# Weight-block sums moved to the input projection, and the start of the output projection rearranged, in a two-layer decoder kernel

## The chip, the core and the metric

The kernel runs on one NeuronCore of a Trainium2 chip. Its engines work side by side, each through its own list of instructions in order: TensorE (PE; PEld are its weight loads), VectorE (DVE), ScalarE (ACT), GpSimd (POOL), and SyncE (SP), which here issues nearly all DMA transfers (SPq is its queue). They wait for one another by semaphores. The metric is the device time of one launch in microseconds, the median of several runs; before the change it is 2179.95 us (2179.53 to 2179.99 in 3 runs).

## The reference

The program is a trunk of two decoder layers over 1024 positions of width 1024, in float32. Layer 0 mixes by latent attention with 12 heads, layer 1 by a sliding window of 128 with 12 query heads and 4 key heads; both have four more heads that attend to a memory of 256 rows.

```
for i in range(DEPTH):
    hn = rmsnorm(x, attn_norm_g[i])
    if i % 2 == 0:
        mix, q_cross = mla_mixer(hn, positions, mla_w_in[j], ..., mla_w_uq[j], mla_w_ukv[j])
    else:
        mix, q_cross = swa_mixer(hn, positions, swa_w_in[j], swa_sinks[j])
    cross = memory_cross_attention(q_cross, mem_n, w_mem_kv[i])
    x = x + jnp.concatenate([mix, cross], axis=-1) @ w_o[i]
    x = x + squared_relu_mlp(rmsnorm(x, mlp_norm_g[i]), mlp_w_up[i], mlp_w_down[i])
return rmsnorm(x, final_norm_g)
```

In the mixer of layer 0, queries come from a product of rank 384 with `mla_w_uq`, of which 64 columns of each head are used as they are and 32 are rotated by position (rope).

## The kernel before

**Products.** A float32 product is made of three fast ones: each operand is split into a high part (a rounding copy, line 99, on ScalarE) and a low part (a subtraction, line 100, on VectorE), and TensorE adds high x high, high x low and low x high in PSUM. A split is thus one operation on ScalarE and, after it, one on VectorE.

**The output projection** `@ w_o` (`wo_phase`) and the MLP use a Strassen-like scheme: 2x2 blocks, seven block products (numbered 1 to 7, done in the order 1, 5, 6, 3, 2, 7, 4), each of which takes sums of blocks as operands. A block product is four steps over the inner dimension (28 steps in all, four PSUM blocks of 128x512 each), and the results go to two sets of four banks, `pswy` (Y) and `pswz` (Z); when a product is complete, VectorE adds the banks to the token tiles (line 1264). The operands of step n are made by `prep(n)`, five steps ahead.

**The weight-block sums** (`wo_sums`, lines 607 to 640) prepare four of the seven weight operands ahead of time and put them, split, into DRAM (`wt_5h`, `wt_5l` and so on). The work is cut into eight quarters. A quarter is 4 loads of w_o (8 in layer 1, whose rows are permuted by head), 4 subtracts (lines 625 to 628), 4 splits and 8 stores. All quarters use one set of four buffers, so the loads of the next quarter wait until the stores of the last have landed. The generator is advanced by `next(summing)` at chosen places:

- in layer 0, two steps for each tile of the values stage (a loop over 8 tiles, in which also the cross attention runs, `pscx`, `pscT`, `psco`) and for each block of the keys (`pskn`); its buffers `wos` are a pool of their own, `wop`, released behind the keys. In the place of `wop` the pool `wu2` opens, with the rope's scratch tiles `ra` and `rb` (lines 299 to 304) and some query weights.
- in layer 1, two steps for each half of a job of the input projection, from the job n = 3 on. A job takes 128 columns of `swa_w_in` (loaded as `wsr`, line 1902; its high and low parts are `wf`). The buffers are the first half of `f1`, which the first score blocks of the window attention (`psw`, with its probabilities `p` in `f1`, line 2009) use next.

**Stages of layer 0, in order of time:** norms and memory products (to about 50 us); the input projection (`psin`, one tile of 128 tokens after another; `psT_a` transposes the normalised tokens, whose split is `xhls`; then the norm of the latent vectors, lines 172 to 184 and 561 to 563, the rope of the key, lines 299 to 304, and `psct` transposes the result); values and cross; keys; the rope queries (`psqr`, then rope on VectorE and POOL, then the transposes `psqt`); attention (`pss`, `pso`); output projection; MLP.

**Around the output projection of layer 0.** The last head's sums of probabilities are handled apart (`LastHead`): ScalarE copies out its denominator and its 64 rows for each half of the tokens (lines 999 and 1002), SP spreads the denominators over partitions, VectorE multiplies. The tokens for the residual come by three groups of loads (line 1202), the first MLP weights by `fill_w` at steps 16 and 18, scaled by ScalarE (line 1362) and split. Behind the last steps the tokens are normalised (`norm`) and transposed (`xT_`).

**What sets the order.** The instructions of each engine are put in order ahead of time by a scheduler that follows the program and the priorities given in it; tiles get their memory from pools, and a new tile waits for the last use of what lay in its place.

## Time and profile before

| | before |
|---|---|
| median of the runs | 2179.95 us |
| the profiled execution | 2177.83 us |
| its span, first to last instruction | 2176.1 us |
| TensorE busy, granted clock | 2080.5 us, 0.982 |
| VectorE busy | 1556.4 us (72%) |
| ScalarE busy | 1149.4 us (53%) |
| GpSimd busy | 161.5 us (7%) |
| HBM read and written | 206.34 MB and 93.63 MB |

The profile is taken from one execution. A row of a timeline has the start and the duration in us, the engine, the line of the kernel, the instruction with output<-input, how many of them, and in brackets the engine's idle time before it and what ended it. What released a wait is inferred from semaphores. The granted clock is the share of its full speed that TensorE was given. A busy engine off the path costs nothing; idle time of TensorE, busy 96% of the span, mostly does.

### The profile page before, as it was taken

To read this page: it belongs to the slowest core of one execution; us is meant where nothing else is said; L and a number is where in the kernel's file an instruction comes from. 1 tells how busy PE (TensorE), PEld (TensorE's weight loads), DVE (VectorE), ACT (ScalarE), POOL (GpSimd) and SP (SyncE) were. 2 spreads that over 40 slices of the span, in tenths; PEclk is the share of its full clock that TensorE was granted. 3 is DMA by queue.
4 is the path that set the end of the run, shared out by engine and by line. 5 is a ranking of instruction groups with operands and counts; after the bars stand their busy time and mean duration, and the time that the engine had idled before them with its cause. 6 is when DMAs were issued, how large, how long until landed. Compare 5 with 4: busy or idle time off the path is not lost.

```text
span 2176.1 us, 29775 instructions
## 1 busy us (share of the span) xinstructions
PE 2080.5 (96%) x9832; PEld 1700.2 (78%) x9832; DVE 1556.4 (72%) x3013; ACT 1149.4 (53%) x2504; POOL 161.5 (7%) x224
## 2 busy tenths in 40 slices
PE   7998699999999999999999999799999999999998
PEld 6987578777777788888888878568778888888887
DVE  7567478867886767795657566687987677886665
ACT  5445367865754444444445453785854444444452
POOL 0012100000100000000001133350000000000000
PEclk9999799999999999999999999899999999999999
DMA  7116323337254445963533235318154445954342
GB/s 250 56 45 184 105 56 94 91 111 242 91 163 147 132 159 174 322 218 114 176 114 112 69 104 155 96 44 285 59 186 139 159 160 176 326 185 145 126 119 90
DMA packets 209797, 314.44 MB, mean 144 GB/s; under 512 B 21629, under 2 KB 101994, under 8 KB 209642
## 3 DMA queue, kind: packets, MB, share of 16 engines
q1 hardware_dynamic: 203200, 296.77, 42.8%
q0 software_dynamic: 4016, 13.12, 1.7%
q10 hardware_dynamic: 2426, 2.65, 0.4%
q8 instruction: 77, 1.26, 0.2%
q14 instruction: 78, 0.64, 0.1%
HBM read 206.34 MB, written 93.63 MB: 138 GB/s over the span
## 4 chain that ended last, share of the span: by engine, by line
PE 60%; DMA 13%; DVE 9%; ACT 5%; issue 2%; SPq 1%; POOL 0%; DVEq 0%; ACTq 0%
PE psy L1799 5%; PE psy L1801 5%; PE psy L1800 5%; DMA mr<-in_mlp_w_up_dram 4%; PE psz L1799 4%; PE psz L1800 4%; PE psz L1801 4%; PE pss L917 4%; PE pso L959 3%; DMA d<-in_mlp_w_up_dram 3%; PE psu L1462 3%; PE psu L1463 3%; PE psu L1464 3%; PE psv L1464 1%; PE psv L1463 1%
## 5 line engine op out<-in xcount | busy, mean ns | idle before, releaser
L1362 ACT ACTIVATE mr<-mr,gcol 128x256 f32<-128x256 f32 (+1 forms) x160 | 67.4, 476 | 83.0 <-DMA mr<-in_mlp_w_up_dram 72.0
L1362 ACT ACTIVATE d<-d,gcol 128x256 f32<-128x256 f32 x128 | 57.2, 498 | 84.1 <-DMA d<-in_mlp_w_up_dram 59.6
L1799 PE MATMUL psy<-g 128*128 128x512 f32 x256 | 99.9, 390 | 0.0
L1800 PE MATMUL psy<-g 128*128 128x512 f32 x256 | 99.6, 389 | 0.0
L1801 PE MATMUL psy<-g 128*128 128x512 f32 x256 | 99.3, 389 | 0.0
L99 ACT ACTIVATE g<-i 128x512 fp32r<-128x512 f32 x79 | 49.6, 628 | 88.0 <-PE psz L1800 45.2
L100 DVE TENSOR_TENSOR g<-i,g 128x512 fp32r<-128x512 f32 x79 | 55.7, 705 | 49.3 <-ACT g L99 49.2
L99 ACT ACTIVATE uh<-i 128x512 fp32r<-128x512 f32 x66 | 41.6, 631 | 85.2 <-PE psy L1800 40.7
L938 ACT ACTIVATE p<-pss 128x512 f32<-128x512 f32 x108 | 63.6, 593 | 43.5 <-PE pss L917 43.4
L99 ACT ACTIVATE i<-mr 128x512 fp32r<-128x512 f32 x78 | 49.0, 628 | 69.0 <-PE psy L1800 20.4
L100 DVE TENSOR_TENSOR pl<-p,ph 128x512 fp32r<-128x512 f32 (+1 forms) x96 | 61.7, 652 | 26.4 <-ACT ph L99 25.9
L789 DVE TENSOR_REDUCE m<-psx 128x1 f32<-128x128 f32 (+5 forms) x96 | 70.3, 749 | 11.1 <-PE psx L785 10.8
L100 DVE TENSOR_TENSOR uh<-i,uh 128x512 fp32r<-128x512 f32 x66 | 45.5, 690 | 45.0 <-ACT uh L99 44.9
L1799 PE MATMUL psz<-g 128*128 128x512 f32 x192 | 74.7, 389 | 0.0
L1800 PE MATMUL psz<-g 128*128 128x512 f32 x192 | 74.7, 389 | 0.0
L1801 PE MATMUL psz<-g 128*128 128x512 f32 x192 | 74.7, 389 | 0.0
L100 DVE TENSOR_TENSOR i<-mr,i 128x512 fp32r<-128x512 f32 x78 | 53.6, 688 | 21.6 <-ACT i L99 21.3
L99 ACT ACTIVATE ph<-p 128x512 fp32r<-128x512 f32 (+1 forms) x96 | 56.4, 599 | 1.3
L1680 DVE TENSOR_TENSOR mqf<-mqq,mqf 128x512 f32<-128x512 f32 x64 | 43.1, 686 | 19.3 <-DMA mqq<-in_mlp_w_down_dram 19.1
L1801 PEld LDWEIGHTS psy<-g 128*128 128x128 f32 x256 | 48.0, 188 | 10.1
L1799 PEld LDWEIGHTS psy<-g 128*128 128x128 f32 x256 | 48.1, 188 | 9.9
L1800 PEld LDWEIGHTS psy<-g 128*128 128x128 f32 x256 | 48.1, 188 | 9.8
(685 smaller groups left out, 7006.2 us busy)
## 6 DMA issues: line engine op xcount, KB each, us to landing
i<-hd SPq DMA_DIRECT2D x154, 256.0 KB
hd<-uh SPq DMA_DIRECT2D x76, 256.0 KB
hd<-ul SPq DMA_DIRECT2D x76, 256.0 KB
mr<-in_mlp_w_up_dram SPq DMA_DIRECT2D x36, 512.0 KB
hd<-x SPq DMA_DIRECT2D x72, 256.0 KB
mr<-hd SPq DMA_DIRECT2D x70, 256.0 KB
d<-in_mlp_w_up_dram SPq DMA_DIRECT2D x32, 512.0 KB
mqq<-in_mlp_w_down_dram SPq DMA_DIRECT2D x32, 512.0 KB
```

The source lines that it names most:

```text
L99: r = nc.scalar.activation(hi, src, AF.Copy)
L100: nc.vector.tensor_tensor(lo, src, f32(hi), ALU.subtract)
L789: nc.vector.reduce_max(m8s[h][:, i : i + 1], ps[:, c], axis=AX, negate=True)
L917: return lambda: nc.tensor.matmul(o, a, b, skip_group_check=True, **kw)
L959: mms.append(lambda: nc.tensor.matmul(o, a, b, skip_group_check=True, **kw))
L1362: nc.scalar.activation(w[:, k, :], w[:, k, :], AF.Copy, scale=g_mlp[layer][:, k0 + k : k0 + k + 1])
L1462: nc.tensor.matmul(ps, wh[:, k, :], xh[:, k, :], start=p in (1, 2, 5) and k == 0, stop=False, skip_group_check=True)
L1463: nc.tensor.matmul(ps, wh[:, k, :], xl[:, k, :], start=False, stop=False, skip_group_check=True)
L1464: nc.tensor.matmul(ps, wl[:, k, :], xh[:, k, :], start=False, stop=k == 3, skip_group_check=True)
L1799: nc.tensor.matmul(ps, ah[:, j, :], bh, start=p in (1, 5, 2) and k == 0, stop=False, skip_group_check=True)
L1800: nc.tensor.matmul(ps, ah[:, j, :], bl, start=False, stop=False, skip_group_check=True)
L1801: nc.tensor.matmul(ps, al[:, j, :], bh, start=False, stop=k == NP - 1, skip_group_check=True)
```

## The change

Four groups of edits:

1. *Sums of layer 0.* They move ahead, into the loop of the input projection (two steps per iteration from the second on), with four buffers and four places for high parts in the second half of `f1`. The pool `wop` goes.
2. *Sums of layer 1.* They start at job 4 instead of 3, with two sets of four buffers in the first half of `f1` and three places for high parts in a small pool `wosp`.
3. *Output projection.* The first two left operands are split before the attention's end (`woa`, in steps 8 and 9 of `WoRaw`). In layer 0, Y takes single banks and Z pairs (the other way round before). The last head's normalisation covers 128 rows at once, instead of 64 here and 64 by `rc_mul(3)`. The token loads `a5` and `u2` move to steps 1 and 6; the first MLP weights are loaded and scaled at steps 2 and 4 instead of 16 and 18, and split at 6 and 14; tokens are normalised at steps 20 and 21 and their first transposes start at step 21. Product 4's weight operands have a tile of their own.
4. *MLP start.* Two transposes instead of three are left to the MLP, and a scaling (`gain_w(0)`) comes behind the last split of the output projection.

```
+    quarters = [f1[:, 2 + i // 4, (i % 4) * 256 : (i % 4) * 256 + 256] for i in range(8)]
+    summing = wo_sums(0, [quarters[0:4]], quarters[4:8])
     a_norm(0)
     for k in range(NT + 2):
+        for _ in range(2 if k else 0):
+            next(summing, None)
...
+        def run():
+            for n in range(ns):
+                load(n)
+            yield
+            for n in range(8):
+                s = sets[n % ns]
+                V(s[0], s[1], s[0], ALU.subtract)
+                V(s[1], s[2], s[1], ALU.subtract)
+                V(s[2], s[2], s[0], ALU.subtract)
+                V(s[3], s[3], s[2], ALU.subtract)
+                put(n, 0)
+                put(n, 1)
+                yield
+                put(n, 2)
+                put(n, 3)
+                if n + ns < 8:
+                    load(n + ns)
+                yield
...
-    wop = pool("wop", "right")
-    summing = wo_sums(0, wop.tile([P, 6, 256], F32, name="wos"))
...
         values_of(t)
-        for _ in range(2):
-            next(summing, None)
...
-        for _ in range(2):
-            next(summing, None)
         nc.vector.tensor_copy(kn[j][:, 0:512], ps[:, 0:512])
...
-    wop.release()
...
+            if n in (8, 9):
+                t_ = quad.tile([P, 2, 512], F32R, tag="raw", bufs=2, name=f"woa{self.layer}_{n}")
+                self.a.append([t_[:, e, :] for e in range(2)])
+                self.his.append(split(self.o[:, 2 * (n - 8), 0:512], *self.a[-1]))
...
-            if n == GRP[c + 1] * NB + LB + 3:
+            if c < 3 and n == GRP[c + 1] * NB + LB + 3:
                 muls = rc_mul(c)
...
         load(a1, 0, 0)
-        load(a5, 1, 1)
-        load(u2, 0, 1)
...
-        for n in range(4):
-            prep(n)
+        with tc.high_priority(offset=150):
+            for n in range(4):
+                prep(n)
         if head:
-            with tc.issue_after(his[1].ins):
+            with tc.issue_after(his[3].ins):
                 head()
...
+        Y, Z = banks("y", layer == 1), banks("z", layer == 0)
...
+            if n == 1:
+                load(a5, 1, 1)
+            if n == 6:
+                load(u2, 0, 1)
...
-            if n in (16, 18):
-                m.fill.append(fill_w(layer, m, n // 2 - 8))
+            if n in (2, 4):
+                fills.append(fill_w(layer, m, n // 2 - 1))
+            if n in (6, 14):
+                m.fill.append(fills[n // 14]())
...
-            if p == 7:
-                norm(n % 4)
+            if n in (20, 21):
+                norm(2 * (n - 20))
+                norm(2 * (n - 20) + 1)
+            if n > 20:
+                xT_(n - 21)
...
-        m.late = [lambda t=t: xT_(t) for t in (5, 6, 7)]
+        m.late = [lambda t=t: xT_(t) for t in (6, 7)]
...
-            if n == 3 and not i:
-                summing = wo_sums(1, f1[:, 0:2, :].rearrange("p a (b c) -> p (a b) c", c=256))
-            for _ in range(2 if n > 2 else 0):
+            if n == 4 and not i:
+                quarters = [f1[:, i_ // 4, (i_ % 4) * 256 : (i_ % 4) * 256 + 256] for i_ in range(8)]
+                wosp = pool("wosp")
+                wos = wosp.tile([P, 3, 256], F32, name="wos")
+                summing = wo_sums(1, [quarters[0:4], quarters[4:8]], [wos[:, e, :] for e in range(3)])
+            for _ in range(2 if n > 3 else 0):
                 next(summing, None)
```

Three places show how the built order of the instructions moves.

VectorE, one tile of layer 0's input projection, before: from the split of the next tile (`xhls`), through the norm's small steps (lines 183, 184), to the normalised tokens (line 201) and latent vectors (561, 562).

```order
L100 TENSOR_TENSOR xhls<-psT_a_0_1092,xhls 128x512
L183 TENSOR_SCALAR ss_1106<-ss_1106 128x1
L183 TENSOR_SCALAR ss_1039<-ss_1039 128x2
L340 SCALAR_TENSOR_TENSOR qc_88<-psct_0_1069,qc_88 64x128
L184 TENSOR_TENSOR rs_1110<-rs_1110,ss_1106 128x1
L184 TENSOR_TENSOR rs_1045<-rs_1045,ss_1039 128x2
L100 TENSOR_TENSOR xhls<-psT_a_4_1099,xhls 128x512
L201 TENSOR_SCALAR fa_86<-fa_86,rs_1110 128x1024
L561 TENSOR_SCALAR fa_87<-psin_990,rs_1045 128x384
L562 TENSOR_SCALAR fa_87<-psin_990,rs_1045 128x256
```

The same place in the changed kernel; lines 620 to 622 are three of the subtracts of the sums, whose quarters are parts of the tile `fa_87`.

```order
L620 TENSOR_TENSOR fa_87<-fa_87 128x256
L183 TENSOR_SCALAR ss_1098<-ss_1098 128x1
L183 TENSOR_SCALAR ss_1007<-ss_1007 128x2
L621 TENSOR_TENSOR fa_87<-fa_87 128x256
L184 TENSOR_TENSOR rs_1102<-rs_1102,ss_1098 128x1
L184 TENSOR_TENSOR rs_1013<-rs_1013,ss_1007 128x2
L340 SCALAR_TENSOR_TENSOR qc_88<-psct_0_1037,qc_88 64x128
L201 TENSOR_SCALAR fa_86<-fa_86,rs_1102 128x1024
L561 TENSOR_SCALAR fa_87<-psin_958,rs_1013 128x384
L562 TENSOR_SCALAR fa_87<-psin_958,rs_1013 128x256
L340 SCALAR_TENSOR_TENSOR qc_88<-psct_0_1037,qc_88 64x128
L622 TENSOR_TENSOR fa_87<-fa_87 128x256
```

Subtracts stand inside the chain of the norm now; the two splits of `xhls` have left it and stand behind the rope that follows these rows.

TensorE at the start of layer 0's output projection, before (with buffer numbers): the last matmul of the attention, then the first blocks of the first product (lines 1258 to 1260); `pswy0_0` is a tile of two banks, so the first two blocks go to it.

```order
L959 MATMUL pso11_0_4962<-pl11_0_3_4973,vh1_2695 128x384
L1258 MATMUL pswy0_0_5084<-wob0_4788,g0_0_13_5043 128x512
L1259 MATMUL pswy0_0_5084<-wob0_4788,g0_0_13_5043 128x512
L1260 MATMUL pswy0_0_5084<-wob0_4788,g0_0_13_5043 128x512
L1258 MATMUL pswy0_0_5084<-wob0_4788,g0_0_13_5043 128x512
```

And in the changed kernel.

```order
L974 MATMUL pso11_0_4963<-pl11_0_3_4974,vh1_2690 128x384
L1285 MATMUL pswy0_0_5069<-wob0_4783,woa0_8_4927 128x512
L1286 MATMUL pswy0_0_5069<-wob0_4783,woa0_8_4927 128x512
L1287 MATMUL pswy0_0_5069<-wob0_4783,woa0_8_4927 128x512
L1285 MATMUL pswy0_1_5070<-wob0_4783,woa0_8_4927 128x512
L1286 MATMUL pswy0_1_5070<-wob0_4783,woa0_8_4927 128x512
L1287 MATMUL pswy0_1_5070<-wob0_4783,woa0_8_4927 128x512
```

The operand is `woa`, split earlier, where it was `g`, split after the attention's last copies of probabilities; each of the four blocks of Y has a tile of one bank.

SP in layer 1's input projection, before: the last `wsr` load (line 1902), with the sixth quarter's loads around it, and that quarter's first stores; two more quarters follow.

```order
L608 DMA fb_10515<-in_w_o_dram 64x256 x2
L1902 DMA wsr_11692<-in_swa_w_in_dram 128x8x128
L603 DMA fb_10515<-in_w_o_dram 128x256 x2
L633 DMA wt_5h<-fb_10515 128x256
L633 DMA wt_7h<-fb_10515 128x256
L633 DMA wt_7l<-fb_10515 128x256
L633 DMA wt_5l<-fb_10515 128x256
```

The last `wsr` load in the changed kernel (line 1947), with the eighth quarter's stores around it; `wor` are the loads of the next stage.

```order
L611 DMA wt_5h<-wos 128x256
L611 DMA wt_5l<-fb_10502 128x256
L611 DMA wt_7h<-wos 128x256
L611 DMA wt_7l<-fb_10502 128x256
L1947 DMA wsr_11709<-in_swa_w_in_dram 128x8x128
L611 DMA wt_6h<-wos 128x256
L611 DMA wt_6l<-fb_10502 128x256
L611 DMA wt_4h<-wos 128x256
L611 DMA wt_4l<-fb_10502 128x256
L590 DMA wor_11936<-in_w_o_dram 64x512 x10
```

All eight quarters stand ahead of or around this load; before, the stores of five did.

More of the change, by code (lines that the diff above doesn't have):

```diff
@@ L1232, in prep @@
             (ah, al), (bh, bl) = slots[n % 8]
-            his.append(split(a, ah, al))
+            if n < 2:
+                ah, al = wo.a[n]
+            else:
+                his.append(split(a, ah, al))
             if p == 1:
@@ L1546, in mlp @@
         go(0, 2, m.fill[0][2])
-        m.late[2]()
-        gain_w(0)
+        with tc.issue_after(m.last_a.ins):
+            gain_w(0)
         sum_w(0)
```

175 lines of the change are left out of this document (92 added, 83 removed).

## The prediction

> **What bounds the kernel now.** I read the page first, then the waits of TensorE by length, then windows of busy time by stage, then the timeline around the longest waits.
>
> ```profile
> PE 2080.5 (96%) x9832; PEld 1700.2 (78%) x9832; DVE 1556.4 (72%) x3013; ACT 1149.4 (53%) x2504; POOL 161.5 (7%) x224
> ```
>
> TensorE is the bound: it is busy 2080.5 of a span of 2176.1 us, so all its gaps together are 95.6 us. The change alters no product, so it can win only from these gaps and from the stretches of reduced clock behind them. The waits (line, what was waited for, total, times, longest) say where the large ones are:
>
> ```profile
> PE psqt L842 <- POOL fa L304: 20.8, 1, 20.8
> PE psw L2004 <- DVE fb L2009: 12.3, 1, 12.3
> PE pswz L1258 <- DVE i L1264: 3.9, 1, 3.9
> PE pswy L1258 <- ACT fa L1002: 2.5, 1, 2.5
> PE pscT L388 <- POOL cps L428: 2.1, 1, 2.1
> PE psco L403 <- DVE cpT L392: 2.1, 2, 1.7
> PE pswy L1260 <- DVE g L100: 2.1, 1, 2.1
> ```
>
> Every one of them but the cross attention's (pscT, psco) lies at a place that the diff names. The windows give the stages (after the names: busy time with instruction counts of PE, PEld, DVE, ACT, POOL; then granted clock, DMA share, GB/s):
>
> ```profile
> 40.00:143.00 103.00, 101.07 (x537) 91.07 (x535) 57.39 (x218) 49.58 (x152) 3.08 (x14) 0.98 0.17 58
> 143.00:216.00 73.00, 62.34 (x370) 52.02 (x369) 57.05 (x116) 44.30 (x135) 17.60 (x12) 0.95 0.53 164
> 1460.00:1476.00 16.00, 13.68 (x59) 10.92 (x59) 15.21 (x26) 8.19 (x14) 0.00 (x0) 1.00 0.89 321
> 1558.00:1594.00 36.00, 31.33 (x130) 24.04 (x131) 32.77 (x55) 23.54 (x48) 0.00 (x0) 1.00 0.36 114
> ```
>
> The input projection (40 to 143) is full on TensorE, with VectorE at 56% and the queues nearly empty. The values and cross stage behind it loses 10.7 us, with VectorE at 78%.
>
> **The change part by part.** All against the profiled execution's 2177.83 us.
>
> *1. The wait of 20.8 us.* The sums of w_o run beside values, cross and keys, and hold SP's queue up to here:
>
> ```profile
> 233.31 0.41 SPq L633 DMA_DIRECT2D wt_4l<-wos  x1
> 235.58 0.36 DVE L300 TENSOR_TENSOR ra<-psqr,sinb 128x192 f32<-128x192 f32 x1 [2.72 <-DMA qk1l<-kl]
> 237.21 0.90 PE L842 MATMUL psqt<-ident,fa 128*128 128x128 f32 x3 [20.78 <-POOL fa L304]
> 237.00:242.00 5.00, 4.79 (x17) 4.70 (x18) 3.98 (x11) 1.27 (x5) 3.00 (x6) 0.50 0.31 100
> ```
>
> The rope's tile `ra` lies in a pool that opens where the sums' pool `wop` closed, so L300 waits until the last stores of the sums have landed; the profile names a late transfer beside them. The changed kernel has no `wop`; by the built order L300 waits there only for its product. Gain 20.8 us, and 5 us at a clock of 0.50 become 2.5. What is late next is the rope weights' own loads, which before stood between the sums' rows and in the changed SP order stand in one block behind the projection: bounds 0 to 20.8 for the wait. The row nearest to L300's time after is its product, finished before the wait began, so the whole wait goes. I take 20.8 + 2.3 = **-23.1**.
>
> *2. Values and cross.* Taken out of 143 to 240, per line (minimum/median/maximum ns):
>
> ```profile
> L100 DVE TENSOR_TENSOR wos<-wos x32: 408/418/1360, 149.1 to 232.4; 128x256 fp32r<-128x256 f32 x32
> L625 DVE TENSOR_TENSOR wos<-wos x8: 415/426/426, 147.1 to 226.0; 128x256 f32<-128x256 f32 x8
> ```
>
> 32 low parts and 4 x 8 subtracts (the other three lines have L625's shape) are 64 x 0.42 = 27 us of VectorE (with as many copies on ScalarE as low parts), in order ahead of the cross's own steps. The 10.7 us of gaps are chains through these two engines, but also through POOL (17.6 us busy), which stays. Bounds 0 to 10.7; I take half, **-5**.
>
> *3. The same work in the input projection.* One quarter per tile adds 8 VectorE operations, 3.4 us, to a tile. Where the tile's slack is:
>
> ```profile
> 91.53 0.93 PE L573 MATMUL psct<-ident,fa 128*128 128x128 f32 x7
> ...
> 100.58 0.22 POOL L304 TENSOR_TENSOR fa<-fa,rb 128x16 f32<-128x16 f32 x1
> 103.33 0.93 PE L573 MATMUL psct<-ident,fa 128*128 128x128 f32 x7
> 75.03 12.12 SPq L485 DMA_DIRECT2D fa<-in_x_dram  x2
> 104.01 1.05 ACT L171 ACTIVATE fa<-fa 128x1024 f32<-128x1024 f32 x1
> 144.22 1.75 SPq L603 DMA_DIRECT2D wos<-in_w_o_dram  x4
> 155.26 2.09 SPq L603 DMA_DIRECT2D wos<-in_w_o_dram  x4
> ```
>
> The rope of a tile is done 2.5 us before TensorE transposes it. In the changed VectorE order three or four subtracts (1.3 to 1.7 us) stand inside that chain, and the split of the next tile (two operations, 1.2 us) moves behind it, so the chain hardly grows; TensorE has the 1.2 us to spare, since the split is used a tile later. The sums' own cycle, load to load, was 11.0 us (144.22 to 155.26) against a tile's 11.8 (91.53 to 103.33), so a quarter fits, with little left. The first quarter is also loaded between the first weights of the projection, when TensorE already waits. Bounds: -1 (the work fits everywhere) and +12 (1.5 us lost on each of eight tiles). The nearer row is the slack of 2.5 us: I take 2 at the start and 2 in the loop, **+4**.
>
> *4. Start of layer 0's output projection.*
>
> ```profile
> 478.76 0.34 PE L959 MATMUL pso<-pl,vh 128*128 128x384 f32 x1
> 481.00 0.59 ACT L1002 ACTIVATE fa<-pso 64x512 f32<-64x512 f32 x1
> 481.64 0.80 PE L1258 MATMUL pswy<-wob,g 128*128 128x512 f32 x1 [2.54 <-ACT fa L1002]
> 481.00:488.00 7.00, 4.30 (x9) 2.98 (x10) 5.62 (x10) 2.45 (x4) 0.00 (x0) 0.52 0.96 304
> 161.70:165.70 4.00, 4.00 (x18) 3.67 (x20) 4.00 (x9) 2.74 (x10) 1.89 (x1) 0.50 0.39 131
> 176.80:180.80 4.00, 3.94 (x28) 3.41 (x29) 2.37 (x6) 3.39 (x14) 1.89 (x1) 1.00 0.55 165
> ```
>
> Before, the first product waits for ScalarE to empty the last attention banks (the copy at 481.00). After, three matmuls of the first block go to a bank that is free, about 0.75 us, and the second block still needs the bank that this last copy empties: about 1.8 us of gap stay. The second wait (2.1 us) goes, since its operands are split before the attention ends. That is 2.5 + 2.1 - 1.8 = 2.8 us. The 4.3 us of matmuls at a clock of 0.52 cost about 2 us more (4.3 x 0.48). Whether they stay slow hangs on 1.8 us: after the gap of 1.7 us (176.8) the clock was 1.00, after those of 2.1 (161.7) and 2.5 it was about half. 1.8 is nearer to 1.7; I take **-4.8**, bounds 0 and -6.6. The Trainium skill, page "TensorE: Matmul & The Clock Gate", section "HAM oscillation — how this bites in real kernels", puts the limit at gaps of about 3.4 us. The rows disagree: 2.1 us was enough. By the page's limit the sum would be the same -4.8, and by a limit just under 1.8 us it would be -2.8.
>
> *5. The wait of 3.9 us between two products on the same banks.*
>
> ```profile
> 530.35 2.09 ACT L1362 ACTIVATE d<-d,gcol 128x256 f32<-128x256 f32 x5
> 533.60 2.48 DVE L1264 TENSOR_TENSOR i<-pswz,i 128x512 f32<-128x512 f32 x4
> ```
>
> The addition at 533.60 that frees the banks stood behind splits whose copies ScalarE made late, since it was scaling MLP weights (five scalings, 2.09 us, in the row at 530.35). By the diff these scalings move fourteen steps of four blocks earlier, where products of the first two groups cover them; if that cover is missing, the 2.1 us of the row show there. Also, a step on the other banks comes between. I take **-3.5**, bounds 0 and -3.9.
>
> *6. Layer 1's sums.*
>
> ```profile
> 1290.47 0.39 SPq L1902 DMA_DIRECT2D wsr<-in_swa_w_in_dram  x1
> 1341.60 0.53 SPq L1902 DMA_DIRECT2D wsr<-in_swa_w_in_dram  x1
> 1344.24 0.33 SPq L633 DMA_DIRECT2D wt_5h<-fb  x1
> 1369.96 0.33 SPq L633 DMA_DIRECT2D wt_5h<-fb  x1
> 1375.98 0.34 SPq L633 DMA_DIRECT2D wt_4l<-fb  x1
> 1377.84 0.47 PE L2004 MATMUL psw<-kh,q 128*128 128x128 f32 x1 [12.30 <-DVE fb L2009]
> 1377.80:1382.80 5.00, 4.96 (x15) 4.20 (x16) 2.10 (x15) 3.22 (x17) 2.78 (x5) 0.54 0.01 3
> ```
>
> The first score block's output lies where the sums' quarters lie, so TensorE waits for the last store (1375.98). A quarter took (1369.96 - 1344.24) / 2 = 12.9 us. By the new order the first store comes behind the weight load of 1290.47, and the last quarter brackets the load of 1341.60. SP then issues about 16 transfers of 0.33 to 0.53 us per quarter, some 7 us; with two sets of buffers the landing times no longer add. Eight quarters end then near 1290 + 8 x 7.5 = 1350 (half a microsecond more for weight loads between), before 1365.5, where TensorE ran out of other work (1377.84 - 12.30). The gap goes, and 2.3 us of half clock (5 x 0.46) with it. Bounds: -14.6 and +20 (second rival). I take **-12**.
>
> *7. The rest.* Token loads moved behind the weight-block loads: the window 1460 to 1476 has 2.3 us of gaps; I take -1.5 (0 to -2.3). MLP weights, transposes and normalisation moved earlier: the gaps 1558 to 1594 (4.7 us) and their like in layer 0 are VectorE chains (VectorE 32.8 of 36 us busy), on which the same operations stand: -1, bounds +3 and -4. The normalisation of the last head is folded into another multiply on the same chain, and bank names change: 0, bounds 1 each way.
>
> Sum: -23.1 - 5 + 4 - 4.8 - 3.5 - 12 - 1.5 - 1 = **-46.9**, so 2130.9 us profiled. The median of the runs is 2.1 above the profiled execution (2179.95 against 2177.83); the forecast is **2133 us**.
>
> **Rivals.** (a) *The projection loses time on every tile*: the new subtracts wait for their loads inside the chain and the slack of 2.5 us is used up; at 1.5 to 2.5 us on eight tiles, +12 to +20 instead of +4: about 2145. For it: the cycle of 11.0 against 11.8 us. Against it: the order moves the split out of the chain.
> (b) *Layer 1's quarters keep their 12.9 us.* Then the last weight load, now behind seven and a half quarters, comes at 1290 + 97 = 1387; with some 10 us for landing and split (an estimate) TensorE goes on at 1397 instead of 1377.8: +20 instead of -12, so 2165. It decides from (1355 - 1290) / 7.5 = 8.7 us per quarter, 1355 being ten before 1365.5. Against it: the second set of buffers.
> (c) *The change doesn't do what it says at psqt*: the rope weights' loads take the sums' place and half of the wait, 10 us, stays (an estimate between its bounds): 2143. Against it: TensorE had its first rope products done before the wait, with the sums' stores still in the queue, and now they are gone from it.
> (d) *Slower*: the tile's chain and the quarter's cycle run one after the other instead of side by side, since the load of an x tile on SP stands behind stores that wait for splits. A tile's chain, from the transposes at 91.53 to the rope's end at 100.8, is 9.3 us; behind the 11.0 of a quarter that makes 20.3, 8.5 over the period, on eight tiles +68 instead of +4: about 2197. It decides from (46.9 + 4) / 8 = 6.4 us per tile. Against it: the x loads are issued early (75.03 and, with the row's 12.12 us, 87 for a use at 104.01). The Trainium skill, "DMA: Bandwidth & Descriptors", section "Anatomy of one DMA — SWDGE (gpsimd) path", says that a semaphore wait is made on the issuing sequencer before dispatch, so all that stands behind it waits too. The SP rows here agree (12.12 us for two x loads).
>
> **How the numbers follow.** Forecast, within 2120 to 2142: 0.62. (a) 0.15, (b) 0.10, (c) 0.08, (d) 0.03; the remaining 0.02 is a gain beyond 2120. Low end 2118: part 2 at -10.7, part 3 at 0, part 7 at its best. High end 2156: (a) and (c) inside, (b) left out. 0.2%, or 4.4 us, is about what a measurement of this kernel tells from no change: faster 0.95, same 0.03 (part of (b) with (a)), slower 0.02.
>
> **What would show it.** Right: no TensorE gap over 3 us between 216 and 245 of before's order; one gap near 1.8 us ahead of the second block of pswy, at full clock; psw of layer 1's first scores without a gap over 3; tiles of the projection at 11.8 us. Wrong: psct waiting for POOL or VectorE in the projection (a), psf waiting for wf in the last job (b), psqr waiting for its weights (c).

## The result, and the profile after

The changed kernel takes 2142.62 us (median of 6 runs, 2138.83 to 2144.53); the kernel before, measured beside it, takes 2179.74 (2172.25 to 2180.41). The ratio is 0.9836, interval [0.9818, 0.9853]. That is 37.1 us faster, where 46.9 had been forecast. The sign holds, and the time lies between the low end of 2118 and the high end of 2156. The size is 10 us short: the time is just outside the span of 2120 to 2142 to which the forecast had given 0.62.

The page's busy times, changed kernel, in the columns of before:

```profile
PE 2070.5 (97%) x9832; PEld 1690.8 (79%) x9832; DVE 1543.8 (72%) x3011; ACT 1150.0 (54%) x2504; POOL 161.9 (8%) x224
```

The span is 2140.5, so TensorE's gaps together are 70.0 us, against 95.6. The products are the same, yet their busy time fell by 10.0 us, since less of it runs at a reduced clock (the mean granted clock of the execution rose from 0.982 to 0.994). The other 25.6 us are gaps. The waits of TensorE in the changed kernel (line, what was waited for, total, times, longest):

```profile
PE psf L109 <- ACT wf L99: 13.8, 3, 6.9
...
PE pswy L1285 <- ACT fa L1017: 1.9, 1, 1.9
...
PE psct L573 <- DVE qc L340: 1.6, 2, 1.0
...
PE pscT L388 <- POOL cps L428: 1.0, 1, 1.0
...
PE pswz L1285 <- DVE i L1291: 0.8, 1, 0.8
```

The 20.8 us at psqt and the 12.3 at psw are gone; psw's largest is 0.9. A new row has taken their place: the projection of layer 1's sliding-window attention waits three times, 13.8 us in all, for its own weights. This is the sign that the prediction named for rival (b).

To see where the gain arises and where it is lost again, here are the starts of the same matmuls in the two profiled executions, and the distance between them:

| first or last matmul of | before | after | ahead by |
|---|---|---|---|
| psin, first (input projection, layer 0) | 46.1 | 47.5 | -1.4 |
| psin, last | 137.7 | 144.6 | -6.9 |
| psqr, first (queries with rope) | 211.5 | 206.3 | 5.2 |
| psqr, last | 249.0 | 220.6 | 28.4 |
| pso, last (attention, layer 0) | 478.8 | 450.2 | 28.6 |
| psu, first (MLP, layer 0) | 597.6 | 557.9 | 39.7 |
| psy, first (second half of that MLP) | 900.3 | 860.4 | 39.9 |
| psf from wsh, last (layer 1, first weights) | 1305.6 | 1262.8 | 42.8 |
| psf from wf, last (last weights) | 1391.1 | 1350.1 | 41.0 |
| pswo, last (attention, layer 1) | 1459.6 | 1420.1 | 39.5 |
| psz, last (MLP, layer 1) | 2124.9 | 2088.2 | 36.7 |
| end of the span | 2176.1 | 2140.5 | 35.6 |

Layer 0 gives nearly everything. Layer 1, where 12 us had been forecast, wins 2.9 until the last matmul on its first weights (`wsh`), gives back 1.8 from there to the last matmul on `wf`, and some microseconds more by the end.

The windows of the first stages show the same in busy time (columns as in the prediction); first before, then after, each cut at the same matmuls:

```profile
46.00:138.00 92.00, 92.00 (x485) 82.91 (x484) 49.73 (x197) 40.65 (x130) 3.08 (x14) 0.99 0.15 47
138.00:211.50 73.50, 62.84 (x377) 52.34 (x376) 58.08 (x123) 45.91 (x143) 17.60 (x12) 0.95 0.47 148
211.50:249.50 38.00, 17.22 (x91) 16.53 (x89) 22.22 (x59) 12.13 (x31) 8.50 (x14) 0.69 0.55 162
```

```profile
46.00:144.60 98.60, 93.21 (x484) 81.82 (x483) 69.53 (x257) 53.56 (x161) 3.20 (x14) 1.00 0.51 161
144.60:206.30 61.70, 59.48 (x378) 50.72 (x377) 37.14 (x80) 38.71 (x122) 17.39 (x12) 1.00 0.20 55
206.30:221.00 14.70, 14.69 (x90) 14.18 (x89) 13.74 (x39) 7.72 (x21) 8.67 (x14) 1.00 0.42 116
```

The projection, which had no gap, now has 5.4 us of them, with VectorE at 71% instead of 54%. The stage of values, cross and keys had 10.7 us of gaps at a mean clock of 0.95; now it has 2.2 at 1.00, with 20.9 us less of VectorE in it. The stage of the long wait has become 38.00 - 14.70 = 23.3 us shorter, and is full.

What happened to layer 1's sums stands in SP's queue. Its rows in the changed kernel: the first store, an early quarter's eight loads and eight stores, and a late part with the weight load (`wsr`) that stands between stores, down to the last store:

```profile
1265.08 0.34 SPq L611 DMA_DIRECT2D wt_5h<-wos  x1
...
1280.38 5.11 SPq L590 DMA_DIRECT2D fb<-in_w_o_dram  x8
1285.59 0.54 SPq L611 DMA_DIRECT2D wt_5h<-wos  x1
1286.22 0.38 SPq L611 DMA_DIRECT2D wt_5l<-fb  x1
...
1289.16 0.40 SPq L611 DMA_DIRECT2D wt_4l<-fb  x1
1289.65 2.39 SPq L590 DMA_DIRECT2D fb<-in_w_o_dram  x4
...
1327.76 0.39 SPq L1947 DMA_DIRECT2D wsr<-in_swa_w_in_dram  x1
...
1331.90 0.32 SPq L611 DMA_DIRECT2D wt_4l<-fb  x1
```

Before, the first of these stores stood here:

```profile
1257.70 0.34 SPq L633 DMA_DIRECT2D wt_5h<-fb  x1
```

From the first store to the last the sums took 1375.98 - 1257.70 = 118.3 us before and 1331.90 - 1265.08 = 66.8 after: the second set of buffers does speed them up, by 51.5 us. But relative to the work around them they begin later. TensorE is 42.8 us ahead at this place, so the old start, moved along, would be 1214.9; the new one is 1265.08, which is 50.2 us late. Pace and start cancel almost exactly, and the queue is still full of the sums while the last three weight loads are to pass through it.

### The profile page after: what moved, and what is told of

Its sections match the earlier page's. It is cut to its first block, busy times and chain, and to the rows that moved or that the text cites. A ratio compares the mean times of both kernels' runs of the same rounds, so it can differ in the third digit from the quotient of the medians.

```text
span 2140.5 us, 29718 instructions
## 1 busy us (share of the span) xinstructions
PE 2070.5 (97%) x9832; PEld 1690.8 (79%) x9832; DVE 1543.8 (72%) x3011; ACT 1150.0 (54%) x2504; POOL 161.9 (8%) x224
## 5 line engine op out<-in xcount | busy, mean ns | idle before, releaser
L100 DVE TENSOR_TENSOR pl<-p,ph 128x512 fp32r<-128x512 f32 (+1 forms) x96 | 61.7, 652 | 25.4 <-ACT ph L99 24.8
L1845 PEld LDWEIGHTS psy<-g 128*128 128x128 f32 x256 | 48.1, 188 | 9.9
L1846 PEld LDWEIGHTS psy<-g 128*128 128x128 f32 x256 | 48.0, 188 | 10.0
L1507 PE MATMUL psu<-g,i 128*128 128x512 f32 x120 | 49.3, 411 | 6.8 <-ACT d L1546 4.1
```

The source lines that it names most:

```text
L100: nc.vector.tensor_tensor(lo, src, f32(hi), ALU.subtract)
L1507: nc.tensor.matmul(ps, wh[:, k, :], xh[:, k, :], start=p in (1, 2, 5) and k == 0, stop=False, skip_group_check=True)
L1845: nc.tensor.matmul(ps, ah[:, j, :], bl, start=False, stop=False, skip_group_check=True)
L1846: nc.tensor.matmul(ps, al[:, j, :], bh, start=False, stop=k == NP - 1, skip_group_check=True)
```

## The experiments

All times below are medians, with the ratio to the kernel before as measured beside them. Its median was 2179.74 us beside the change, 2176.21 beside e1 to e4, 2177.93 beside e5 to e8, and 2175.17 beside e9 to e12. It moves by up to 4.6 us from one group to the next, so between groups the ratios compare better than the medians do. Repeats of one kernel spread over 1 to 10 us, so differences of 2 or 3 us between two experiments are not told apart by them; where a stage matters it is read from the trace.

| kernel | time, us | ratio [95%] |
|---|---|---|
| the change | 2142.62 | 0.9836 [0.9818, 0.9853] |
| e1 weight loads on POOL's queue | 2140.58 | 0.9841 [0.9826, 0.9857] |
| e2 fewer, larger loads | 2182.42 | 1.0032 [1.0019, 1.0046] |
| e3 layer 1's sums as before | 2142.69 | 0.9855 [0.9835, 0.9874] |
| e4 layer 0's sums as before | 2168.84 | 0.9963 [0.995, 0.9977] |
| e5 layer 1's sums a job earlier | 2130.71 | 0.9786 [0.9762, 0.981] |
| e6 e5 and e1 | 2127.24 | 0.9778 [0.9753, 0.9802] |
| e7 layer 0's subtracts on POOL | 2137.0 | 0.9825 [0.9796, 0.9853] |
| e8 MLP weights late again | 2136.36 | 0.9817 [0.9796, 0.9838] |
| e9 banks as before | 2144.22 | 0.9862 [0.9837, 0.9886] |
| e10 no early operands | 2134.83 | 0.9817 [0.9793, 0.9841] |
| e11 e8 and e9 | 2143.03 | 0.9859 [0.9829, 0.9889] |
| e12 earlier start with the output kept, and e7 | 2130.91 | 0.9801 [0.9776, 0.9826] |

### e1: the late weight loads leave SP's queue

```
-            nc.sync.dma_start(out=raw, in_=wsv[:, :, c0 : c0 + P])
+            (nc.sync if wf is None else nc.gpsimd).dma_start(out=raw, in_=wsv[:, :, c0 : c0 + P])
```

> The weight loads of layer 1's last six jobs (wsr) are issued by POOL instead of SP; nothing else changes. Theory Q (these loads stand in SP's queue behind the sums' transfers): the three waits of psf for wf (13.8 us) fall below 2 us, the half clock behind them goes, time about 2127 (15 less than the changed kernel's 2142.6). Rival S (ScalarE and VectorE are late with the split of the weights, whatever the queue): the waits stay above 10 us, time about 2142.

The weight loads do come earlier (the last is issued at 1294.87 instead of 1327.76), but the time is not told apart from the changed kernel's, so neither expectation holds: the waits at psf fall, and another comes. The waits of TensorE in e1:

```profile
PE psw L2049 <- DVE fb L2054: 7.0, 1, 7.0
...
PE psf L111 <- DVE wf L100: 3.9, 1, 3.9
```

And the last store of its sums:

```profile
1332.73 0.32 SPq L611 DMA_DIRECT2D wt_4l<-fb  x1
```

The wait has moved back to where it was before the change (psw, whose output lies where the quarters lie), because the sums end at 1332.73 as they did at 1331.90. So the place of the weight loads is one face of the loss, and the late end of the sums the other; taking away one face shows the other.

### e2: the same bytes in fewer transfers

```
-        for g in range(2):
-            h = 3 * (2 * a + g) + e
-            nc.sync.dma_start(out=dst[g * 64 : g * 64 + 64], in_=w_o[layer, h * 64 : h * 64 + 64, cols])
+        h = 6 * a + e
+        src = w_o[layer, 384 * a : 384 * a + 384, cols].rearrange("(g q) c -> g q c", g=2)[:, 64 * e : 64 * e + 64, :]
+        nc.sync.dma_start(out=dst, in_=src)
```

> The two 64-row loads of the permuted rows of w_o in layer 1 are one transfer of 128 rows: 4 loads per quarter instead of 8 or 6. Theory Q with SP bound by the issue of transfers (loads about 0.62 us each): a quarter of 16 transfers falls from 9.2 to about 6.7 us, the waits of psf fall from 13.8 to about 5, time about 2133. If the landing of the transfers sets the pace: quarters stay at 9, time within 2 of 2142.

Two loads of 64 rows become one of 128, for the sums and also for the raw weights of layer 1's output projection, which the same function loads. It was meant to shorten the queue and did the opposite: the kernel is slower than before the change. TensorE waits 22.9 us for `wf` at psf, in two waits, and 7.7 us for a load of `wt_6h` in layer 1's output projection. Rows of its SP queue:

```profile
1278.76 2.28 SPq L590 DMA_DIRECT2D fb<-in_w_o_dram  x3
1281.09 2.73 SPq L611 DMA_DIRECT2D wt_5l<-fb  x1
...
1290.35 4.84 SPq L590 DMA_DIRECT2D fb<-in_w_o_dram  x3
1295.24 2.59 SPq L611 DMA_DIRECT2D wt_5h<-wos  x1
```

The queue has fewer loads, but stores that took 0.3 to 0.5 us take 2.4 to 3.3 in four places of the first quarters, right behind such loads. The run says nothing for or against the queue as the bound, since the transfers themselves changed. The Trainium skill, "DMA: Bandwidth & Descriptors", section "Why a DMA increments its semaphore by 16 and not by 1", states a rule that bears on it: the number of DMA engines that share a transfer goes by its slowest dimension, which is 2 in the merged source. The longer rows fit that, and so does the DMA engines' busy share between 1278 and 1300 us, which is 0.1 to 0.2 in 25 of 40 slices (two busy engines of 16 are 0.125); which engines worked was not seen.

### e3 and e4: each layer's sums as before, the rest changed

e3 gives layer 1 back the old function with one set of buffers and the start at job 3; e4 gives layer 0 back its pool and its places in values and keys. From the edit of e3:

```
-            if n == 4 and not i:
...
-                summing = wo_sums(1, [quarters[0:4], quarters[4:8]], [wos[:, e, :] for e in range(3)])
+            if n == 3 and not i:
+                summing = wo_sums1(1, f1[:, 0:2, :].rearrange("p a (b c) -> p (a b) c", c=256))
```

> Of the change, the part on layer 1's sums alone is undone (one set of buffers, start at job 3). The forecast's sixth term (-12): 2154 or more. Theory Q (12.3 us of waiting for the score block were exchanged for 13.8 of waiting for weights): within 3 us of 2142.

> Of the change, the move of layer 0's sums alone is undone (pool wop, steps in the values and keys loops). By the forecast's terms 1 to 3 (-23.1 - 5 + 4): +24, about 2167. By the stages of the two traces (-23.2 - 12.1 + 6.9): +28, about 2171. The wait of about 20 us at psqt comes back in both.

e3 takes the time of the changed kernel, to a tenth of a microsecond in the median; by the ratios it is 0.9855 against 0.9836, with intervals that overlap. The largest wait of its TensorE is the old one (psg's 9.7 us, at the start of layer 0, are in all these kernels):

```profile
PE psw L2076 <- DVE fb L2081: 11.7, 1, 11.7
```

and of e4's:

```profile
PE psqt L887 <- POOL fa L304: 20.3, 1, 20.3
```

So the edit of layer 1's sums brings nothing that these runs tell from zero: it exchanges 11.7 us at psw for 13.8 at psf. The move of layer 0's sums is worth 2168.84 - 2142.62 = 26.2 us (27.6 by the ratios). That is most of the whole gain.

### e5 and e6: layer 1's sums start one job earlier

```
-            if n == 4 and not i:
+            if n == 3 and not i:
...
-                summing = wo_sums(1, [...], [wos[:, e, :] for e in range(3)])
+                summing = wo_sums(1, [...], [f1[:, 2, e * 256 : e * 256 + 256] for e in range(3)])
-            for _ in range(2 if n > 3 else 0):
+            for _ in range(2 if n > 2 else 0):
```

The high parts lie in a part of `f1` instead of `wosp`. It holds the output of layer 1's cross-attention, which they overwrite, so e5 and e6 show only what the earlier start does to the time. e6 also has the edit of e1.

> Layer 1's sums start at job 3 again, as before the change, but keep their two sets of buffers (the places for high parts lie in a part of f1 that is free there). Theory P (the sums end at the same time as before because they start some 31 us later, though a quarter takes 8.9 us instead of 12.9): first store near 1240, last near 1312 instead of 1332; the three waits of psf fall from 13.8 to 7 or less, no wait at psw, time about 2135. Theory Q alone (only the weight loads' place in the queue counts; they still stand behind six quarters): the waits of psf stay at about 14, time about 2142.

> As e5, and the weight loads of the last six jobs are issued by POOL. Theory P: neither psf nor psw waits over 2 us, time about 2127. If the sums end late whatever their start, as in e1 (7.0 at psw): about 2140.

Both waits are gone: in e5 no row of psf from wf is left among the larger ones, and psw's is 1.1 us. The first and the last store of the sums in e5:

```profile
1217.80 0.34 SPq L611 DMA_DIRECT2D wt_5h<-fb  x1
...
1303.17 0.32 SPq L611 DMA_DIRECT2D wt_4l<-fb  x1
```

The start is 47.3 us earlier than in the changed kernel, the end 28.7, and the last matmul from `wf` starts at 1335.6 instead of 1350.1. The kernel is 11.9 us faster in the median (10.9 by the ratios), and the intervals of the ratios do not overlap. This is about the 12 us that term 6 had forecast. With the earlier start, the queue of the weight loads no longer matters (e6: 1336.1). The two runs together show that the late start was what cancelled the second set of buffers.

The late start also has a good side. From the first to the last matmul on `wsh`, while layer 1's cross-attention still runs, TensorE takes 96.5 us before, 97.2 in e3, 96.8 in e5 and 98.8 in e6, which all start the sums at job 3; it takes 93.4 in the changed kernel and 93.4 to 93.8 in e1, e4 and e7 to e12. (e12 starts at job 3 too, but its first store comes 82 us into this stage; before it was 49 us, in e5 50.5.) Over the whole stage, from the first matmul on `wsh` to the last on `wf`, the times are 182.0 us before, 180.7 after, 183.4 in e3, 168.3 in e5 and 173.7 in e12.

### e7: layer 0's subtracts on POOL

```
-        V, ct, ns = nc.vector.tensor_tensor, [0], len(sets)
+        V, ct, ns = (nc.vector if layer else nc.gpsimd).tensor_tensor, [0], len(sets)
```

> The 32 subtracts of layer 0's sums run on POOL instead of VectorE. Theory V (the projection's 5.5 us of loss come from the subtracts standing in VectorE's chain): the waits of psct and psT_a in the projection fall to under 1.5 us, time 2139. Rival W: POOL waits for the sums' loads ahead of the rope's two steps, so psct waits longer: 2146 or more.

In this run the loop of the projection has no gap left: the waits of psct and psT_a in it are 0.4 us in all. The time from the first to the last psin is 93.2 us (49.4 to 142.6), against 97.1 in the changed kernel and 91.6 before. The groups of one subtract line in layer 0 (instruction, duration in ns as minimum/median/maximum, first and last start), of the changed kernel and of e7:

```profile
L619 DVE TENSOR_TENSOR fa<-fa x8: 418/426/426, 39.0 to 138.6; 128x256 f32<-128x256 f32 x8
```

```profile
L619 POOL TENSOR_TENSOR fa<-fa x8: 729/738/923, 35.3 to 123.9; 128x256 f32<-128x256 f32 x8
```

A subtract takes 738 ns instead of 426, on an engine that is nearly idle there, and the gaps are gone; so they came from the chain through VectorE. How much time that wins is less sure than 97.1 against 93.2 suggests. The ten profiles with all of these subtracts in the projection and on VectorE (the change, e1 to e3, e5, e6, e8 to e11) have 94.9 to 97.1 us from the first to the last psin; the two with POOL (e7, e12) have 93.2 and 93.1. That is a gain of 1.7 to 4 us in the loop. But the loop also starts later in these two, at 49.4 and 50.9 against 46.7 to 49.0, and it ends at 142.6 and 144.0, within the 142.5 to 145.0 of the others. In the total, e7 is not told apart from the changed kernel.

### e8, e9 and e11: what removed the wait of 3.9 us at pswz

e8 puts the loading and scaling of the MLP weights back to steps 16 and 18, e9 gives Y pairs of banks and Z single ones again in layer 0, e11 does both.

```
-            if n in (2, 4): ...
-            if n in (6, 14): ...
+            if n in (16, 18): m.fill.append(fill_w(layer, m, n // 2 - 8)())
```

```
-        Y, Z = banks("y", layer == 1), banks("z", layer == 0)
+        Y, Z = banks("y", True), banks("z", False)
```

> Of the change, the MLP weights' move is undone: loaded, scaled and split at steps 16 and 18. The forecast's fifth term: +3.5, about 2146, with a wait of 3 to 4 us at pswz back. If the bank swap alone removed that wait: within 2 of 2142.6.

> Of the change, the bank swap of layer 0 alone is undone (Y in two pairs, Z in four single banks). Theory B (the swap removed the 3.9 us wait between products 3 and 2, since e8 left it away without the early weights): a wait of 3 to 4 us at pswz is back, time up to 4 us more than the changed kernel. Forecast's theory (the early scaling removed it): no such wait. At the start of the projection Y's first pair waits for the last attention bank from its first matmul on: one gap of about 2.5 us instead of 1.9.

> The bank swap and the early MLP weights both undone. Theory B: as e9, a wait of 3 to 4 us at pswz. If either edit alone suffices: the wait is here (3 to 4 us), and not in e8 and not in e9.

The wait of 3.9 us stays away in all three: pswz waits at most 1.0 us (e11). So neither early scaling nor the other banks, alone or together, is what removed it. The banks do something else. With the old ones the transposes for the MLP wait, and it starts 4.4 us later (562.3 against 557.9):

```profile
PE psT_m L1330 <- ACT x L1336: 4.6, 5, 1.4
```

What removed the 3.9 us stays open, but the traces name a candidate. Before, ScalarE had a pause of only 0.25 us between 519.8 and the late copy at 532.35, and what it scaled in the last 6 us of this were not the first MLP weights of `fill_w` (128x128 each, done by then) but two later groups of MLP weights, in tiles of 128x256. Two rows before, and the first of the same group in e11:

```profile
526.49 0.91 ACT L1362 ACTIVATE mr<-mr,gcol 128x256 f32<-128x256 f32 x2 [0.25 <-DMA mr<-in_mlp_w_up_dram]
527.83 0.89 ACT L1362 ACTIVATE mr<-mr,gcol 128x256 f32<-128x256 f32 x2
```

```profile
510.39 0.49 ACT L1401 ACTIVATE mr<-mr,gcol 128x256 f32<-128x256 f32 x1
```

This group is the scaling `gain_w(0)` of the fourth group of edits, which puts it behind the last split of the output projection. It stays there in e8, e9 and e11: in e11 it begins 15.9 us after the addition (at 494.49) that frees the banks, where before four of its scalings (1.80 us) stood ahead. No run undoes this edit alone, nor the higher priority of the first operands, the moved token loads and the earlier normalisation, so none of them is shown to be the cause.

### e10: no early operands

```
-            if n in (8, 9):
+            if False:
```

> Of the change, the early split of the first two left operands is undone. Forecast's fourth term: a second wait of about 2 us behind the first one at pswy, with half clock behind it: +2 to +4.8 us. If the high priority of the first four preparations covers it: no second wait, within 2 us of 2142.6.

The start of layer 0's output projection in the changed kernel (timeline: start, duration, and in brackets the idle time before and what ended it), and the window around it:

```profile
453.12 0.50 PE L1285 MATMUL pswy<-wob,woa 128*128 128x512 f32 x1 [1.88 <-ACT fa L1017]
```

```profile
450.00:456.00 6.00, 4.12 (x20) 3.10 (x19) 6.00 (x11) 4.04 (x8) 0.00 (x0) 1.00 0.78 253
```

and the same two views of e10:

```profile
451.24 0.50 PE L1284 MATMUL pswy<-wob,g 128*128 128x512 f32 x1 [0.78 <-DVE g L100]
```

```profile
450.00:456.00 6.00, 5.22 (x23) 3.99 (x23) 6.00 (x10) 5.07 (x9) 0.00 (x0) 1.00 0.76 236
```

Without the early operands the wait for a copy out of the attention's banks (1.88 us) is gone. The wait that is left, 0.78 us, is of the second kind: for the low part of `g`, as the 2.06 us before. The MLP starts 3.5 us earlier (554.4). So most of the second wait was removed by something else than the early operands, and they cost more here than they save. The raised priority of the first operands is a candidate; it was not tried by itself, and the banks, the last head's normalisation and the token loads were changed too.

### e12: an earlier start that overwrites nothing

The high parts of the first steps at job 3 lie in a tile of the MLP, `uh`, that is free by then; from job 4 on they go to `wosp`. Nothing is overwritten. The subtracts of layer 0 stand on POOL, as in e7.

```
+            if n == 3 and not i:
+                t_ = m0.t("uh")
+                wohi = [t_[:, e // 2, (e % 2) * 256 : (e % 2) * 256 + 256] for e in range(3)]
+                summing = wo_sums(1, [quarters[0:4], quarters[4:8]], wohi)
             if n == 4 and not i:
                 wos = wosp.tile([P, 3, 256], F32, name="wos")
+                wohi[:] = [wos[:, e, :] for e in range(3)]
-            for _ in range(2 if n > 3 else 0):
+            for _ in range(2 if n > 2 else 0):
```

> The changed kernel with layer 1's sums started at job 3 (two sets; the first places for high parts in a weight tile of the MLP's pool that is free then) and layer 0's subtracts on POOL. From e5 (-12) and e7 (3 to 4 us in the projection): no wait over 3 us at psf or psw, time about 2127; the ratio to the kernel before about 0.976.

It takes 2130.91 us, 0.9801 of before. That is 11.7 less than the changed kernel in the median, but 7.6 by the ratios, and the intervals of the two ratios overlap a little (0.9818 to 0.9826), so its gain over the changed kernel rests on the stage above (173.7 against 180.7 us) more than on the total. The expectation of no wait over 3 us at psf fails. One large weight wait is left, since the loads still stand in SP's queue with the sums:

```profile
1302.54 0.79 PE L109 MATMUL psf<-xnh,wf 128*128 128x512 f32 x1 [7.82 <-ACT wf L99]
```

Its first store comes at 1248.51, between e5's 1217.80 and the changed kernel's 1265.08, right behind the copy on ScalarE that makes its operand (1248.07, 0.42 us). The lead that e6 has over it is within the spread.

## Why the prediction was right in sign and range, and 10 us off in size

| term | forecast | measured | by |
|---|---|---|---|
| 1 wait at psqt | -23.1 | -23.2 | psqr, first to last: 37.5 to 14.3 |
| 2 values and cross | -5 | -12.1 | psin last to psqr first: 73.8 to 61.7 |
| 3 sums in the projection | +4 | +6.9 | psin last, 6.9 later |
| 4 and 5, start of the output projection to the MLP, layer 0 | -8.3 | -11.1 | pso last to psu first: 118.8 to 107.7 |
| 6 layer 1's sums | -12 | +1.8 | psf, wsh last to wf last: 85.5 to 87.3 |
| 7 and the rest | -2.5 | +2.1 | what is left of -35.6 |

The terms sum to -46.9 in the forecast and -35.6 in the trace. That they come within 11 us of each other is partly luck: terms 2, 4 and 5 came out 9.9 us better than forecast and terms 3, 6 and 7 21.3 us worse, so half of what was lost was hidden by what was not expected. The time alone would also have pointed at the wrong rival: 2142.6 is nearer to (c) at 2143 and (a) at 2145 than to the forecast of 2133, and yet the stages show that (c) did not occur and (a) only in small.

**Term 1** is right in mechanism and size: the wait is gone whole, the rope weights' loads did not take its place (rival (c) fell), and e4 shows both that the wait returns with the old place of the sums and that the move is worth 26 to 28 us, with terms 2 and 3 in it.

**Term 2** was right in mechanism, but its size was less than half of what came, and the result lies beyond its bound of 10.7. The forecast took half of 10.7 us because the chains also run through POOL. POOL's busy time is the same (17.60 and 17.39), but 8.5 us of the gaps go, and TensorE's busy time in the stage falls by 3.4 us since its clock is now 1.00. POOL had merely been in the chains; VectorE and ScalarE made them long. The 3.4 us of clock are what puts the result beyond the bound: the prediction had the clock of 0.95 in its window, but counted only gaps.

**Term 3** was right in its place and low by 3 us. The step that failed is that the chain "hardly grows". Moving the split out of the chain did not free what the subtracts put in: the loop grew by 5.5 us, some 0.7 per tile, against the forecast's 2 (3.3 to 5.5 in the ten profiles of this loop). With the subtracts off VectorE (e7) its gaps go. The sign named for rival (a) did show: psct waits for VectorE 1.6 us and for POOL 1.4. So (a)'s mechanism occurred, below its price of 12 to 20. Rival (d) fell.

**Term 4** came out at -4.95 (from the last pso to the first matmul of the second step, 10.04 us before and 5.09 after): the first gap is 1.88 us for a forecast 1.8, the second wait is gone, and the clock stayed at 1.00, as chosen from the row with a gap of 1.7. Yet two of its reasons fell. The second wait does not hang on the operands being split early (e10), and that edit costs 1.1 us in the place. And the choice of the clock by the length of the gap was luck. The other traces show no limit between 1.7 and 2.1 us. A longer gap in the changed kernel kept the full clock, and in e8 a gap as long as the forecast one did not (gap, and the 4 us from it):

```profile
1338.13 0.50 PE L109 MATMUL psf<-xnh,wf 128*128 128x512 f32 x1 [2.23 <-ACT wf L99]
1338.10:1342.10 4.00, 3.97 (x19) 3.28 (x20) 2.73 (x7) 1.86 (x7) 0.39 (x1) 1.00 0.00 0
```

```profile
545.48 1.61 PE L1330 MATMUL psT_m<-ident,i 128*128 128x128 f32 x8 [1.87 <-ACT i L1319]
545.40:549.40 4.00, 3.92 (x15) 3.39 (x16) 4.00 (x8) 3.82 (x9) 0.00 (x0) 0.57 0.00 0
```

**Term 5** has its wait gone (3.9 to 0.8), but by neither of the two causes that the prediction gave (e8, e9, e11). It had also misread its row: the five scalings at 530.35 are of the group `gain_w(1)` (tile `d`, 128x256), which the diff does not move; in the changed kernel they stand at 491.14 to 497.3, just ahead of the same addition again. The right number with the wrong reason would have misled anyone who went on from it. In the same stage, a part that was put at nothing (bank names change: 0) was worth more than this term: with the old banks the stage from pso to psu takes 113.3 us (e9) and 113.0 (e11), with the new ones 107.7 (107.2 to 109.1 in e1, e3 to e8 and e12).

**Term 6** is the step that cost the forecast its 12 us. Three statements in it failed. First, the start: "the first store comes behind the weight load of 1290.47". Moved along by 42.8 us, that is 1247.7. The order is as it said, and that load is issued at 1248.68; but the store does not follow at once. It came at 1265.08, 17.4 us after 1247.7. It did not wait for a queue place but for a copy. SP's waits in the changed kernel, and ScalarE's timeline there:

```profile
SPq L611 <- ACT wos L99: 21.1, 7, 16.3
```

```profile
1264.03 0.59 ACT L333 ACTIVATE kh<-psf 64x512 fp32r<-64x512 f32 x1
1264.64 1.03 ACT L99 ACTIVATE wos<-fb 128x256 fp32r<-128x256 f32 x3
```

The copies of the high parts stand on ScalarE behind those of the key job (`kh`), and nothing in the prediction looked at ScalarE's order there. Second, the pace: 16 transfers at 0.33 to 0.53 us are not 7 us. Eight loads alone took 5.11 us in the row at 1280.38 (0.64 each), and the quarter from there to 1289.56 took 9.2. That is over the 8.7 us from which rival (b) was said to decide. Third, the forecast asked only when the sums end, and not what stands behind them in the same queue, though rival (b) named it: the weight loads of the last three jobs came late between the quarters, and TensorE went on 7.7 to 10.4 us after each (rival (b) had estimated 10). So rival (b)'s mechanism occurred at a milder price, 13.8 us in three waits instead of 20 beyond the old wait. The clock adds to it. Windows of the changed kernel around the three waits (6.92, 4.69 and 2.23 us, in this order):

```profile
1262.00:1303.00 41.00, 34.08 (x152) 27.89 (x150) 26.80 (x48) 17.49 (x35) 14.03 (x31) 0.95 0.54 168
1303.00:1322.00 19.00, 14.31 (x61) 11.75 (x62) 12.86 (x24) 7.60 (x16) 1.89 (x1) 0.86 0.64 200
1322.00:1340.00 18.00, 15.77 (x66) 12.77 (x66) 10.79 (x32) 7.99 (x24) 4.16 (x7) 0.87 0.45 138
```

The granted clock is 0.86 on the mean behind the first wait and still 0.87 a window later. Which of the three statements decided can be worked out and is borne out by e5. TensorE needed the sums by 1365.5 - 42.8 = 1322.7. Starting at 1247.7 with the pace as measured (66.8 us from the first store to the last) they would have ended at 1314.5, in time; starting at 1265.08 with the forecast's 60 us, at 1325.1, too late (both are estimates from these rows). In e5, with the start at job 3 and no faster pace (85.4 us from the first store to the last), the 12 us are there.

**Term 7** was small and stays unsettled. What is won until the last matmul on `wsh` belongs to term 6, since it goes with the start of layer 1's sums (e3, e5, e6); counted from the first matmul on `wsh`, term 6 is -1.3 (182.0 to 180.7) and the rest +5.2. Of the rest, 1.5 us are lost between the last psf and the last pswo, 2.8 in layer 1's MLP and 1.1 at the end; no run took them apart.

## What to carry to other kernels

Work in the background has a start and a pace, and what mostly counts is its end (here an early start also cost the work beside it 3 to 5 us). A change that doubles the buffers and moves the start (here by one job) must be judged by start plus pace, with the in-order engines that stand before its first step (here ScalarE's copies behind the key job) and with everything that shares its queue behind it. When such work ends too late, the wait shows at whichever consumer comes first: taking that consumer out of the way (e1) moves the wait without shortening it, and moving the start removes it (e5) or, moved by less, a part of it (e12: 8.3 us instead of 13.8).

## What the runs showed of the hardware

- A transfer takes up more of SP's queue than had been read off: 0.64 us for a load of 64 rows, about 0.4 for a store of 128 (rows at 1280.38 and 1286.22), and up to 3.3 for a store right behind the joined loads (e2). In the quarter from 1280.38 to 1289.56 the rows stand end to end, so there the queue set the pace.
- Joining two loads into one with a source of three dimensions made the kernel 1.9% slower than the same kernel with the separate loads (2182.42 against 2142.62).
- A subtract of 128x256 float32 took 738 ns on POOL and 426 on VectorE. Where VectorE is in the chain and POOL is nearly idle, the slower engine still shortened the loop (93.2 and 93.1 us against 94.9 to 97.1).
- In gaps of about 2 us, the length alone does not say whether the clock falls. Mean granted clock over the 4 us from the first matmul behind a gap: 0.63 after 1.83 us (e3, at 1246.87), 0.57 after 1.87 (e8, at 545.48), but 1.00 after 1.87 at the same place in the changed kernel (545.57), and 1.00 after 2.23 and 2.48 (changed kernel, at 1338.13 and 1552.97). Before the change it fell to about half after 2.1 and 2.5.
